# A hand-planned order of work, re-planned with measured paces, hops and buffer times, in a one-layer decoder kernel

## The chip, the cores and the metric

The kernel runs on one core of a Trainium2 chip. The metric is the device time of one execution in microseconds (us); smaller is better. The engines are TensorE (PE, matrix products into PSUM), VectorE (DVE), ScalarE (ACT), GpSimd (POOL) and SyncE (SP, which issues most DMAs). Each engine works through its own queue in order; engines wait for each other through semaphores.

## The reference

One layer of a hybrid decoder on x (256 tokens x 2048 features, float32) with 256 memory tokens:

```python
h = rmsnorm(x, norm_mix_g)
proj = h @ w_in + b_in               # GLU input | q | k | v | conv gate | attention gate
y_conv = swish(layernorm(depthwise_causal_conv31(a * sigmoid(g)))) @ w_conv_out
y_att = moba_attention(q, k, v) @ w_att_out      # 8 heads; 256 tokens are one block: plain causal
x = x + (sigmoid(g_conv) * y_conv + sigmoid(g_att) * y_att) @ w_out
x = x + cross_attention(rmsnorm(x), rmsnorm(mem), w_cq, w_ckv, w_co)      # 4 heads of 512
x = x + swiglu(rmsnorm(x), w_ffn_in, w_ffn_out)  # 5632 hidden
return rmsnorm(x, norm_final_g)
```

## The kernel before

**Products.** Every large product is made of 128-row pieces of the contraction. A value in float32 is split into hi and lo (both in the reduced form that PE multiplies at full pace), and a product of a 128x128 left piece and a 128x512 weight piece is three matmuls: hi·hi, hi·lo, lo·hi (`mm3`, lines 290 to 292). In what follows "product" means such a three.

**Blocks, units, pairs.** The work on weights is a list of blocks of 1024 output columns: glu0, glu1, k, q, v, gate10, gate11, ao0, ao1, gate00, gate01, co0, co1, wo0, wo1, cq0, cq1, ck0, ck1, cv0, cv1, xo0, xo1, ffn0 to ffn10, fo0, fo1. A block runs over pairs of contraction pieces (8 pairs; ao and co 4; fo 22). One pair of one block is a unit: 1 MB of weights, loaded by two DMAs (four for two column ranges) on SP (`load_unit`), in a buffer of 128 x 2048. A pair is of one of two kinds:
- W: 2 x 2 x 2 = 8 products. ACT casts the 2048 columns to hi, DVE subtracts to lo.
- S: the same 2x2 block product with 7 products (Winograd's form of Strassen's scheme). DVE makes sums of the weights (1024, 512 and 512 columns), ACT casts 1536 and 2048 columns, DVE subtracts as many. The left side needs sums as well (`make_extra`). S products use other PSUM banks, and `share` folds them into a result block, to which the W part is added in `finish`.

88 of 300 pairs are S: in glu1, k, q, v, gate00, gate01, wo, cq, xo two each, in ck and cv three, in ffn three and four by turns, in fo 6 and 8.

**The planner.** The program is written out by a Python planner that keeps a clock per engine: `t["pe"]`, `t["dve"]`, `t["act"]`, `t["dma"]`. `Timed` wraps DVE and ACT and adds each instruction's assumed cost to its clock; `product` adds 0.681 to PE's clock. After each product, `pump` writes out for DVE and ACT whatever, by these clocks, would start by then (`step`): tasks from a queue (evacuations, softmax and so on), the next weight step in order (`act_step`, `dve_step`), or a tap of the convolution. The order so written is the order of each engine's queue. Tasks are Python generators that yield the engine they want next, or a delay and a number of PSUM banks. PE's queue, too, holds its transposes and attention products where the planner thought that their inputs would be there.

What this planner assumes: a result is usable by another engine at the moment its cost ends; a buffer is free as soon as its release is written out (`Store.free`); a unit lands 2.0 us after a DMA clock that advances by 3.8 per unit; cost depends on the number of elements only.

**Memory.** 25 buffers of 128 x 2048 floats serve as weights (raw, hi, lo, sums) and for everything else, in pieces of a quarter, a half or a whole. `ROOM` says per block how many are kept from the weights.

**The convolution and the layer norm.** Each of 31 taps for each half of the channels is four ACT multiplications into a half buffer and one DVE addition into y (`Conv`). Taps fill idle time; they take priority if they are behind an even pace that ends at `CONV_END` = 350. Then `layer_norm` runs: sums on DVE and PE, squares and Sqrt on ACT, a reciprocal, Silu on ACT, and the split that co0 and co1 multiply. Its steps are ordinary tasks.

**The start.** `begin` loads unit 0 in four pieces; `split_first` casts and subtracts two pieces before product 0 and two before product 4. x comes in eight transposed pieces (`x_load`, `x_make`), and again by rows for the norm (`x_norm`).

Of the kernel before, what the change touches and what calls it, by code (L numbers as in the profile page):

```python
# [46 lines left out]
PRODUCT = 0.681  # L47


class Timed:  # L50
# [5 lines left out]
    def __getattr__(self, name):  # L56
        f = getattr(self._engine, name)
        if name == "dma_start":
            return f

        def call(out, *args, **kwargs):
            t, key = self._clock, self._key
            us = self._cost(math.prod(out.shape[1:]))
            t[key] = t["last"] = max(t[key], t["from"]) + us
            t["busy", key] += us
            return f(out, *args, **kwargs)  # L66
# [12 lines left out]
class Piece:  # L79
    def __init__(self, block, first, n):  # L80
        self.block, self.first, self.n = block, first, n


class Store:
# [3 lines left out]
    def __init__(self, pool, n):  # L88
        self.pool, self.n = pool, n
        self.blocks = []  # L90
        self.made = 0
# [4 lines left out]
    def take(self, n, kind):  # L96
        for b in self.blocks if n < 4 else ():
            if b["kind"] == kind:
                for f in range(0, 4, n):
                    if not any(b["used"][f : f + n]):  # L100
                        b["used"][f : f + n] = [True] * n
                        return Piece(b, f, n)
        assert self.whole() > 0, "no room"
        self.made += 1
        t = self.pool.tile([P, 4, 512], kind, tag="blk", name=f"blk_{self.made}")
        b = {"kind": kind, "tile": t, "used": [i < n for i in range(4)]}
        self.blocks.append(b)
        return Piece(b, 0, n)

    def free(self, pg):  # L110
        b = pg.block
        for x in range(pg.first, pg.first + pg.n):
            assert b["used"][x]
            b["used"][x] = False
        if not any(b["used"]):
            self.blocks.remove(b)

# [13 lines left out]
def ordered(pairs, s, how="first"):  # L131

    rest = [p for p in range(pairs) if p not in s]
    order = []
    for p in s:
        order.append(("S", p))
        if how == "turns":
            order.append(("W", rest.pop(0)))
    return order + [("W", p) for p in rest]


class Builder:
# [4 lines left out]
    def __init__(self, ctx, tc, args):  # L147
        self.tc, self.nc = tc, tc.nc
        self.t = {"pe": 0.0, "dve": 0.0, "act": 0.0, "dma": 0.0, "from": 0.0, "last": 0.0}
# [14 lines left out]
        self.seq, self.tasks, self.queue = 0, [], {"act": [], "dve": []}  # L164
        self.left, self.ready = {}, set()
# [10 lines left out]
    def take(self, n, kind=F32):  # L176
        pg = self.store.take(n, kind)
        if self.blk:
# [3 lines left out]
    def free(self, pg):  # L182
        self.store.free(pg)
# [26 lines left out]

    def run(self, task, ready=None):
        t = self.t
        t["last"] = t["from"] = t["pe"] if ready is None else ready
        try:
# [4 lines left out]
        if isinstance(cmd, str):  # L219
            heapq.heappush(self.queue[cmd], (t["last"], self.seq, task))  # L220
        else:
            delay, banks = cmd
            heapq.heappush(self.tasks, (t["last"] + delay, self.seq, banks, task))
# [22 lines left out]
    def flush(self):  # L246
        while self.tasks or any(self.queue.values()):
# [34 lines left out]
    def pe_add(self, us):  # L282
        self.t["pe"] += us
        self.t["last"] = self.t["pe"]

# [154 lines left out]
    def free_w(self, pg):  # L440
        self.held -= 1
        self.free(pg)
# [28 lines left out]
    def act_cand(self):  # L471
        if self.i_act >= len(self.acts):
            return None
        u, k = self.acts[self.i_act]
        if k == "b":
            if u not in self.sums:
                return None
            at = self.sums[u][1]
# [4 lines left out]
        return at if self.slots() >= 2 + self.owed else None  # L483

    def act_step(self):
        t = self.t
        u, k = self.acts[self.i_act]
        n = 3 if k == "a" else 4
        hi = self.take_w()
        src = self.f32(self.sums[u][0]) if k == "b" else self.f32(self.raw[u])[:, 4 - n :, :]  # L490
        self.act.copy(self.f32r(hi, 0, n), src)
        self.w[u, k] = (hi, None, n)
        self.owed += 1
        self.cast_at[u, k] = t["act"]
# [12 lines left out]
    def dve_step(self):
        t, dve = self.t, self.dve
        u, k = self.dves[self.i_dve]
        if k == "s":  # L510
            r = self.f32(self.raw[u])
            pg = self.take_w(F32)
            s = self.f32(pg)
            dve.tensor_tensor(s[:, 0:2, :], r[:, 0:1, :].to_broadcast([P, 2, 512]), r[:, 1:3, :], op=ALU.add)
            dve.tensor_tensor(s[:, 2, :], s[:, 0, :], r[:, 2, :], op=ALU.add)
            dve.tensor_tensor(s[:, 3, :], s[:, 2, :], r[:, 3, :], op=ALU.add)
            self.sums[u] = pg, t["dve"]
        else:
            hi, _, n = self.w[u, k]
            src = self.sums.pop(u)[0] if k == "b" else self.raw.pop(u)  # L520
# [3 lines left out]
            dve.tensor_tensor(self.f32r(lo, 4 - n), self.f32(src, 4 - n), self.f32(hi, 0, n), op=ALU.subtract)  # L524
            self.free_w(src)
            self.landed[u, k] = t["dve"]
            if k != "a":
                self.prepared = u + 1
        self.i_dve += 1

    def step(self, limit):
# [28 lines left out]
        if what == "task":  # L560
            self.run(heapq.heappop(self.queue[e])[2], r)
# [11 lines left out]
    def advance(self, u, k):  # L573
        while (u, k) not in self.landed:
            assert self.step(1e8), (u, k, self.units[u][0].name, self.slots())
        self.stall("w", self.landed[u, k] - self.t["pe"])

# [19 lines left out]
    def product(self, key, lhs, rhs):  # L597
# [3 lines left out]
        if n == 0:  # L601
            while self.busy[i]:
                assert self.step(1e8), key
# [3 lines left out]
        t = self.t  # L607
        t["pe"] += PRODUCT
# [4 lines left out]
    def pair_w(self, blk, u, p, how):  # L613
# [11 lines left out]
        for x, (i, t, n) in enumerate(order):  # L625
            if how == "start" and x in (0, 4):
                self.split_first(x // 4)
# [55 lines left out]
    def split_first(self, j):  # L683
        hi, lo, _ = self.w[0, "W"]
        for i in range(2):
            x = 2 * i + j
# [3 lines left out]
        if j:  # L690
            self.free_w(self.raw.pop(0))

    def begin(self):
# [9 lines left out]
        self.i_act = self.i_dve = self.n_load = 1  # L703
        self.prepared = 1
        self.load_more()

    def stream(self, blocks, on_load=None):
        self.units = [(blk, kind, p) for blk in blocks for kind, p in blk.order]
        self.acts = [(u, k) for u, (_, kind, _) in enumerate(self.units) for k in ("W" if kind == "W" else "ab")]
        self.dves = [(u, k) for u, (_, kind, _) in enumerate(self.units) for k in ("W" if kind == "W" else "sab")]  # L710
        self.raw, self.w, self.landed, self.loaded, self.cast_at, self.sums = {}, {}, {}, {}, {}, {}
        self.on_load = on_load
# [45 lines left out]
class Conv:  # L758
# [5 lines left out]
    def __init__(self, b, vt, y, t0, t1, done):  # L764
# [4 lines left out]
        self.n = 0  # L769

# [3 lines left out]
    def act_ready(self):  # L774
        if not self.todo or len(self.made) >= self.BUFS:
            return None
        return self.at.get(self.todo[0][0])

    def act_step(self):
        b = self.b  # L780
        h, j = self.todo.pop(0)
        sh = TAPS - 1 - j
        pg = None if sh == 0 else b.take(2)
# [11 lines left out]
        else:  # L795
            self.made.append((h, sh, pg, b.t["act"]))
# [4 lines left out]
    def dve_step(self):  # L801
# [4 lines left out]
        b.free(pg)  # L806
        self.n += 1
        if not self.todo and not self.made:
            b.conv = None
# [3 lines left out]
S_X = [0, 1]  # L813
# [797 lines left out]
```

## Time and profile before

| | before |
|---|---|
| time, median of 3 runs (lowest, highest) | 1761.01 us (1756.18, 1761.41) |
| the profiled execution: time, span | 1759.83 us, 1758.1 us |
| PE busy | 1687.7 us (96%) |
| DVE busy | 1479.7 us (84%) |
| ACT busy | 1013.6 us (58%) |
| HBM traffic | 351 MB, 200 GB/s over the span |
| mean granted clock of TensorE | 0.984 |

How to read it: the span runs from the first to the last instruction; the time of an execution is a little longer. A busy PE is one with a matmul in its pipeline, so short bubbles between matmuls do not show as idle. In the rows of instructions, `L66` is the wrapper line of the planner's DVE and ACT calls, so that groups there are told apart by operation and shape; `blk` is any of the 25 buffers, `psum` the PSUM tile. `[1.27 <-ACT blk L66]` behind a row means that the engine stood idle for 1.27 us before it and that an ACT instruction on `blk` ended the wait. The granted clock is a share of TensorE's full speed.

### The profile page before, as it was taken

To read this page: it belongs to the slowest core of one execution; us is meant where nothing else is said; L and a number is where in the kernel's file an instruction comes from. 1 tells how busy PE (TensorE), PEld (TensorE's weight loads), DVE (VectorE), ACT (ScalarE), POOL (GpSimd) and SP (SyncE) were. 2 spreads that over 40 slices of the span, in tenths; PEclk is the share of its full clock that TensorE was granted. 3 is DMA by queue.
4 is the path that set the end of the run, shared out by engine and by line. 5 is a ranking of instruction groups with operands and counts; after the bars stand their busy time and mean duration, and the time that the engine had idled before them with its cause. 6 is when DMAs were issued, how large, how long until landed. Compare 5 with 4: busy or idle time off the path is not lost.

```text
span 1758.1 us, 20236 instructions
## 1 busy us (share of the span) xinstructions
PE 1687.7 (96%) x7566; PEld 1385.4 (79%) x7566; DVE 1479.7 (84%) x1326; ACT 1013.6 (58%) x1064; POOL 1.4 (0%) x11
## 2 busy tenths in 40 slices
PE   8988899889999999999999999999999999999997
PEld 6876677678888888878888887888888788888776
DVE  5987789857778887898888899999898989887896
ACT  7775588764454456656555465655555555553552
POOL 0000000000000000000000000000000000000000
PEclk9999899999999999999999999999999999999999
DMA  9743364355584676554546665757566657667672
GB/s 343 259 168 132 132 203 156 120 173 174 202 284 143 234 240 205 191 177 168 192 136 201 229 204 180 253 191 246 188 222 199 221 191 275 214 217 226 209 234 90
DMA packets 129987, 352.53 MB, mean 201 GB/s; under 512 B 14433, under 2 KB 14561, under 8 KB 129889
## 3 DMA queue, kind: packets, MB, share of 16 engines
q1 hardware_dynamic: 126864, 341.11, 57.8%
q10 hardware_dynamic: 3024, 10.13, 1.5%
q8 instruction: 59, 0.97, 0.2%
q14 instruction: 40, 0.32, 0.0%
HBM read 339.65 MB, written 11.53 MB: 200 GB/s over the span
## 4 chain that ended last, share of the span: by engine, by line
PE 66%; DVE 15%; ACT 7%; issue 6%; DMA 4%; SPq 1%; DVEq 0%; ACTq 0%
PE psum L290 21%; PE psum L291 21%; PE psum L292 21%; DVE blk L66 15%; ACT blk L66 7%; DMA blk<-in_w_in 2%; PE psum L396 1%; DMA blk<-in_w_ffn_in 1%; DMA md<-blk 0%; DVE mx L66 0%; ACT L66 0%; DMA blk<-in_x 0%; SPq L455 0%; ACT junk L66 0%; SPq L456 0%
## 5 line engine op out<-in xcount | busy, mean ns | idle before, releaser
L66 DVE TENSOR_TENSOR blk<-blk,blk 128x2048 fp32r<-128x2048 f32 (+13 forms) x745 | 1105.4, 1514 | 161.0 <-ACT blk L66 142.1
L290 PE MATMUL psum<-blk,blk 128*128 128x512 f32 x2376 | 934.1, 393 | 28.5 <-DVE blk L66 23.1
L66 ACT CAST blk<-blk 128x2048 fp32r<-128x2048 f32 (+3 forms) x446 | 732.9, 1682 | 348.0 <-DVE blk L66 225.4
L291 PE MATMUL psum<-blk,blk 128*128 128x512 f32 x2376 | 925.5, 390 | 6.9 <-DVE blk L66 6.9
L292 PE MATMUL psum<-blk,blk 128*128 128x512 f32 x2376 | 924.5, 389 | 2.3 <-DVE blk L66 2.3
L290 PEld LDWEIGHTS psum<-blk,blk 128*128 128x128 f32 x2376 | 450.7, 190 | 126.1 <-DVE blk L66 26.0
L291 PEld LDWEIGHTS psum<-blk,blk 128*128 128x128 f32 x2376 | 450.8, 190 | 98.4 <-DVE blk L66 9.9
L292 PEld LDWEIGHTS psum<-blk,blk 128*128 128x128 f32 x2376 | 450.0, 189 | 95.5 <-DVE blk L66 3.6
L66 DVE TENSOR_TENSOR blk<-psum,blk 128x512 f32<-128x512 f32 (+4 forms) x249 | 188.5, 765 | 68.1 <-PE psum L292 64.0
L66 ACT ACTIVATE blk<-blk,vecs 128x256 f32<-128x256 f32 (+31 forms) x290 | 121.0, 494 | 59.2 <-DVE blk L66 55.6
L66 DVE TENSOR_TENSOR blk<-blk 128x1024 f32<-128x1024 f32 (+3 forms) x147 | 131.9, 899 | 8.8 <-DMA md<-blk 5.9
L66 ACT ACTIVATE blk<-blk,rss 128x512 f32<-128x512 f32 x30 | 21.7, 724 | 93.5 <-DVE blk L66 93.5
L66 ACT COPY blk<-psum 128x512 f32<-128x512 f32 (+2 forms) x56 | 38.9, 695 | 50.8 <-PE psum L396 41.5
L396 PE MATMUL psum<-consts,blk 128*128 128x128 f32 x312 | 46.4, 282 | 10.2 <-DVE blk L66 7.9
L396 PEld LDWEIGHTS psum<-consts,blk 128*128 128x128 f32 x312 | 36.3, 142 | 22.3 <-DVE blk L66 15.2
L66 ACT ACTIVATE junk<-blk 128x512 f32<-128x512 f32 x32 | 20.2, 630 | 51.8 <-DVE blk L66 46.6
L66 ACT ACTIVATE blk<-blk 128x512 f32<-128x512 f32 (+1 forms) x26 | 18.8, 729 | 40.0 <-DVE blk L66 35.1
L66 ACT ACTIVATE blk<-blk,rm 128x512 f32<-128x512 f32 (+1 forms) x16 | 11.6, 723 | 37.7 <-DVE blk L66 37.6
L66 ACT CAST blk<-psum 128x1024 fp32r<-128x1024 f32 (+2 forms) x30 | 20.7, 697 | 19.1 <-PE psum L396 14.5
L66 ACT ACTIVATE blk<-psum,mx 128x256 f32<-128x256 f32 (+1 forms) x24 | 10.3, 435 | 18.1 <-DVE mx L66 16.1
L66 ACT ACT_TABLE_LOAD x13 | 16.7, 1283 | 6.0 <-DVE mx L66 4.2
L66 DVE SCALAR_TENSOR_TENSOR blk<-blk,rss 128x512 f32<-128x512 f32 x22 | 16.5, 751 | 3.5 <-ACT blk L66 2.5
(66 smaller groups left out, 147.9 us busy)
## 6 DMA issues: line engine op xcount, KB each, us to landing
blk<-in_w_ffn_in SPq DMA_DIRECT2D x352, 256.0 KB, 4.3
blk<-in_w_in SPq DMA_DIRECT2D x112, 512.0 KB, 4.6
blk<-in_w_ffn_out SPq DMA_DIRECT2D x88, 512.0 KB, 5.0
blk<-in_w_ckv SPq DMA_DIRECT2D x64, 512.0 KB, 4.5
blk<-in_w_in SPq DMA_DIRECT2D x64, 256.0 KB, 5.2
blk<-in_w_out SPq DMA_DIRECT2D x32, 512.0 KB, 5.0
blk<-in_w_cq SPq DMA_DIRECT2D x32, 512.0 KB, 6.0
blk<-in_w_co SPq DMA_DIRECT2D x32, 512.0 KB, 5.6
```

Of the source, the lines that this page charges most:

```text
L66: return f(out, *args, **kwargs)
L290: mm(out, lhs[0], rhs[0], start=start, stop=False)
L291: mm(out, lhs[0], rhs[1], start=False, stop=False)
L292: mm(out, lhs[1], rhs[0], start=False, stop=stop)
L396: self.nc.tensor.transpose(out[:, 2 * c + t, :], src(c, t), self.ident)
```

## The change

The numbers of the planner, its rules, and the list of S pairs are changed. The arithmetic is not, apart from which pairs are made with seven products.

- Costs by kind of instruction, start to start; 0.15 (`HOP`) between engines; 0.12 (`AGAIN`) where an instruction reads what the one before it on its engine wrote; ACT's table loads 1.3; a product 0.6825; a DMA unit 2.5, landing at the earliest 2.6 after its issue.
- `Store` keeps for each piece and each free buffer the time at which it is really released (`at`, `rest`), and work that takes a buffer starts no earlier on the clock. The convolution holds two fixed half buffers and is asked only when the older one is free.
- The three sums of an S unit are three steps; units 1 and 2 are cast and subtracted in halves; unit 0 is split in one go ahead of everything else.
- A third queue, `low`: the steps of the layer norm, which yield to others until `LN_DUE` = 385 and go first after it. `CONV_END` is 375.
- Evacuations count results instead of trusting that (t, n) = (1, 1) is the last, and wait for what they use (`until`).
- S pairs are listed per block (`PLAN`), 94 instead of 88: gate11 one, wo1, cq1 and xo0 three, cv1 two, ffn 3 4 4 3 4 4 3 4 4 4 4. On x's side the S pairs are 2 and 3 instead of 0 and 1, and their sums are made in one go at planner time 30 (`x_extra`).
- The rows of x for the norm are loaded from planner time 14 on in steps of 2.5 (before: from 8 in steps of 3).

```diff
-PRODUCT = 0.681
+PRODUCT = 0.6825
+HOP = 0.15
+AGAIN = 0.12
+AHEAD = (0, 0, 0)
+LOOK = 1
+HALVES = 2
+SLACK = 5.0
...
         def call(out, *args, **kwargs):
             t, key = self._clock, self._key
-            us = self._cost(math.prod(out.shape[1:]))
+            us = self._cost(t, name, out, args, kwargs)
+            ins = [x for x in args if isinstance(x, bass.AP)]
+            if t[key, "wrote"] and any(overlap(t[key, "wrote"], x) for x in ins):
+                us += AGAIN
+            t[key, "wrote"] = out
...
-def dve_cost(n):
-    return 0.066 + 0.0010417 * n
+def dve_cost(t, name, out, args, kwargs):
+    n = size(out)
+    if name in ("tensor_scalar", "tensor_scalar_mul"):
+        return 0.072 + 0.00064 * n
+    if name in ("tensor_reduce", "reduce_max", "reduce_sum"):
+        return 0.1 + 0.0011 * size(args[0])
+    return 0.075 + 0.00104 * n + (0.06 if name == "scalar_tensor_tensor" else 0.0)
...
-def act_cost(n):
-    return 0.22 + 0.00057 * n if n <= 512 else 0.09 + 0.00085 * n
+def act_cost(t, name, out, args, kwargs):
+    n = size(out)
+    if name != "activation":
+        return 0.1 + 0.000835 * n
+    us = 0.183 + 0.00085 * n if n <= 256 else 0.1 + 0.00084 * n
...
+    table = TABLE.get(args[1])
+    if table and table != t["table"]:
+        t["table"] = table
+        us += 1.3
...
     def take(self, n, kind=F32):
         pg = self.store.take(n, kind)
+        self.t["from"] = max(self.t["from"], pg.at)
...
-            t["dma"] = max(t["dma"], t["pe"]) + 3.8
-            self.loaded[v] = t["dma"] + 2.0
+            t["dma"] = max(t["dma"], max(t["pe"], self.raw[v].at) + 2.6) + 2.5
+            self.loaded[v] = t["dma"]
...
+    def parts(self, u, n):
+        return [slice(0, 2), slice(2, 4)] if u <= HALVES else [slice(0, n)]
...
+        for h in self.parts(u, n):
+            self.act.copy(self.f32r(hi)[:, h, :], src[:, h, :])
...
+            if self.low[e]:
+                r = self.low[e][0][0]
+                ways.append((max(now, r) + (-0.4 if t["pe"] > self.low_due else 1.0), r, "low"))
...
     def drop_w(self, u, k):
         hi, lo, _ = self.w.pop((u, k))
-        self.free_w(hi)
-        self.free_w(lo)
+        for pg in (hi, lo):
+            self.free_w(pg, self.t["pe"] + HOP)
...
     def act_ready(self):
-        if not self.todo or len(self.made) >= self.BUFS:
+        if not self.todo or self.pages == [] or self.todo[0][0] not in self.at:
             return None
-        return self.at.get(self.todo[0][0])
+        return max(self.at[self.todo[0][0]], self.pages[0][0] if self.pages else 0.0)
...
+PLAN = {
+    "glu1": "SSWWWWWW", "k": "SSWWWWWW", "q": "SSWWWWWW", "v": "SSWWWWWW", "gate00": "SSWWWWWW",
+    "gate01": "SSWWWWWW", "wo0": "SSWWWWWW", "wo1": "SSSWWWWW", "cq0": "SSWWWWWW", "cq1": "SSSWWWWW",
+    "xo0": "SSSWWWWW", "xo1": "SSWWWWWW", "gate10": "WWWWWWWW", "gate11": "SWWWWWWW", "ck0": "SSSWWWWW",
+    "ck1": "SSSWWWWW", "cv0": "SSSWWWWW", "cv1": "SSWWWWWW", "ffn0": "SSSWWWWW", "ffn1": "SSSSWWWW",
+    "ffn2": "SSSSWWWW", "ffn3": "SSSWWWWW", "ffn4": "SSSSWWWW", "ffn5": "SSSSWWWW", "ffn6": "SSSWWWWW",
+    "ffn7": "SSSSWWWW", "ffn8": "SSSSWWWW", "ffn9": "WSSSSWWW", "ffn10": "SSSSWWWW",
+}
...
-CONV_END = 350.0
+X_EXTRA = 30.0
+X_NORM = 14.0
+CONV_END = 375.0
+LN_DUE = 385.0
```

More of the change, by code (lines that the diff above doesn't have):

```diff
@@ L180, in take, with free @@
         return pg
-    def free(self, pg):
-        self.store.free(pg)
+    def free(self, pg, at=None):
+        self.store.free(pg, self.t["last"] if at is None else at)
     def get(self, pg, lo=0, n=None):
@@ L213, in run @@
         t["last"] = t["from"] = t["pe"] if ready is None else ready
+        t["by"] = "pe" if ready is None else ""
         try:
@@ new lines, in dve_ready @@
+    def dve_ready(self, u, k, ahead):
+        more = 2 if ahead else 0
+        if k == "1":
+            if u >= self.n_load or self.slots() < 1 + self.owed + more:
+                return None
+            return max(self.loaded[u], self.store.rest[0])
+        if k in "23":
+            return self.summed.get((u, int(k) - 1))
+        if self.slots() < 1 or (u, k) not in self.cast_at:
+            return None
+        return max(self.cast_at[u, k], self.store.rest[0])
+    def dve_cand(self):
+        self.dve_at = self.pick(self.dves, self.dve_ready, max(self.t["dve"], self.t["pe"]), "dve")
+        return self.dve_at and self.dve_at[1]
@@ L559, in step @@
         was, t["from"] = t["from"], r
-        if what == "task":
-            self.run(heapq.heappop(self.queue[e])[2], r)
+        if what in ("task", "low"):
+            self.run(heapq.heappop((self.queue if what == "task" else self.low)[e])[2], r)
         elif what == "weights":
@@ L805, in dve_step, with ordered, union @@
         b.dve.tensor_tensor(yy, yy, b.f32(pg).rearrange("p j (c s) -> p (j c) s", s=S)[:, :, sh:S], op=ALU.add)
-        b.free(pg)
+        self.pages.append((b.t["dve"] + HOP, pg))
         self.n += 1
         if not self.todo and not self.made:
+            for _, pg in self.pages:
+                b.free(pg)
             b.conv = None
             b.run(self.done())
-S_X = [0, 1]
-S_MG = [0, 1]
-S_X2 = [0, 1]
-S_M = [0, 1, 2]
-S_CA = [0, 1]
-S_X3 = [0, 1, 2, 3]
+PLAN = {
[6 rows of a table added]
+}
+X_SIDE = ("glu1", "k", "q", "v", "gate10", "gate11", "gate00", "gate01")
+M_SIDE = ("ck0", "ck1", "cv0", "cv1")
+X3_SIDE = tuple(f"ffn{j}" for j in range(11))
+def ordered(name):
+    kinds = PLAN[name]
+    if name not in X_SIDE + M_SIDE + X3_SIDE:
+        return [(k, i) for i, k in enumerate(kinds)]
+    first = 2 if name in X_SIDE else 0
+    rank = [(i + first) % 8 for i in range(8)]
+    s = rank[: kinds.count("S")]
+    w = [p for p in range(8) if p not in s]
+    return [(k, (s if k == "S" else w).pop(0)) for k in kinds]
+def union(*names):
+    return sorted({p for n in names for k, p in ordered(n) if k == "S"})
 S_MID = [3, 6, 9, 12, 15, 18]
@@ L821 @@
 S_BACK = [18, 15, 12, 10, 8, 6, 4, 2]
-HOW = {}
 def setup(b):
@@ L854, in layer, with last_of, until @@
     st = {}
+    S_X = union(*X_SIDE)
+    S_MG, S_X2, S_CA = union("wo0", "wo1"), union("cq0", "cq1"), union("xo0", "xo1")
+    S_M, S_X3 = union(*M_SIDE), union(*X3_SIDE)
     half = lambda ap: ap.rearrange("p j n -> p (j n)")
+    counts = {}
+    def last_of(n, *key):
+        counts[key] = counts.get(key, 0) + 1
+        return counts[key] == n
+    def until(*keys):
+        while any(k not in b.ready for k in keys):
+            yield 0.3, 0
     by_s = lambda ap: half(ap).rearrange("p (f s) -> p f s", s=P)
+    x_kept = {}
     def x_load(p):
-        pg, t = b.page(P)
+        if p in S_X:
+            if "x" not in x_kept:
+                x_kept["x"] = b.take(2 if len(S_X) <= 2 else 4)
+            pg, t = None, b.f32(x_kept["x"])[:, S_X.index(p), :].rearrange("p (a b) -> p a b", b=P)
+        else:
+            pg, t = b.page(P)
         nc.sync.dma_start(t.rearrange("p (k t) s -> p k (t s)", k=2), a["x_t"][:, 2 * p : 2 * p + 2, :])
+        b.t["dma"] += 0.65
         return pg, t
@@ L992, in moba @@
         yield 2 + MOBA_GAP * h, 0
-        while ("kq", h // 4) not in b.ready:
-            yield 1, 0
+        yield from until(("kq", h // 4))
         yield 0, 1
@@ L1145, in evac @@
             done()
+            b.ready.add(("att", t, q))
         w = a["w_att_out"]
@@ L1287, in cross @@
     def cross(h):
+        yield from until(*((x, p) for x in "qk" for p in (2 * h, 2 * h + 1)))
         yield 1, 1
@@ L1345, in cross_out @@
     def cross_out(h):
-        while ("pt", h) not in b.ready:
-            yield 1, 0
+        yield from until(("pt", h))
         for x in range(2):
@@ L1382, in evac @@
                 act.activation(s, ps, AF.Silu, scale=r)
+                b.ready.add(("silu", j, t))
                 return
+            yield from until(("silu", j, t))
             yield "dve"
             dve.scalar_tensor_tensor(s, ps, r, s, op0=ALU.mult, op1=ALU.mult)
-            if t == 1:
+            if last_of(2, "ffn", j):
                 b.run(tr(), b.t["dve"])
```

293 lines of the change are left out of this document (180 added, 113 removed).

## The prediction

> **What bounds the kernel now.** I read the page's totals first, then the stages, then single stalls. TensorE (PE) is the bound by its total:
>
> ```profile
> span 1758.1 us, 20236 instructions
> PE 1687.7 (96%) x7566; PEld 1385.4 (79%) x7566; DVE 1479.7 (84%) x1326; ACT 1013.6 (58%) x1064; POOL 1.4 (0%) x11
> ```
>
> The 96% is an average and hides where PE waits. So I cut the span at block starts, found by counting matmuls of 512 columns (a block of eight pairs with s S pairs is 64-s products of three matmuls). The view of windows gives, after the times, busy us of PE, PEld, DVE, ACT and POOL, then granted clock, DMA share and GB/s:
>
> ```profile
> 6.08:57.86 51.78, 47.63 (x192) 37.82 (x193) 39.08 (x44) 40.23 (x58) 0.00 (x0) 0.93 0.91 334
> 57.86:391.58 333.72, 296.70 (x1270) 238.85 (x1268) 271.31 (x270) 237.63 (x392) 0.00 (x0) 0.94 0.49 164
> 391.58:519.42 127.84, 127.84 (x565) 105.89 (x564) 95.92 (x71) 60.11 (x40) 0.00 (x0) 1.00 0.64 222
> 519.42:1037.87 518.45, 510.77 (x2410) 422.70 (x2409) 439.86 (x400) 292.05 (x282) 0.00 (x0) 1.00 0.57 191
> 1037.87:1510.42 472.55, 465.99 (x2095) 384.66 (x2094) 434.88 (x356) 259.65 (x192) 0.00 (x0) 1.00 0.64 217
> 1510.42:1758.05 247.63, 234.58 (x1023) 191.54 (x1021) 197.79 (x186) 120.98 (x98) 0.00 (x0) 0.98 0.62 199
> ...
> 1086.00:1127.69 41.69, 41.69 (x189) 34.61 (x188) 39.17 (x30) 22.72 (x15) 0.00 (x0) 1.00 0.62 215
> ...
> 1339.55:1383.30 43.75, 41.93 (x189) 34.59 (x188) 41.28 (x34) 23.34 (x16) 0.00 (x0) 1.00 0.62 204
> ```
>
> The third row is the yardstick. From ao0 to gate01 there are 32+32+62+62 = 188 products and nothing else on PE: 127.84/188 = 0.680 us each, with no wait at all. ffn1 (the row from 1086.00) has 60 products, 40.8 us, and one wide transpose: 0.88 us for that, 0.11 for each block of 128 columns. With these two prices every other stage splits into work and loss:
> - glu0 (6.08 to 57.86): 64 products, 43.5; lost 8.3.
> - glu1 to gate11 (57.86 to 391.58): 376 products, 255.7; six wide transposes, 5.3; eight attention heads of 15 column blocks, 13.2; column sums, 0.5. Sum 274.7; lost 59.0.
> - co0 to xo1: 680 products, 462.4; 20 wide transposes, 17.6; cross attention and its sums, 25.4. Lost 13.
> - ffn0 to ffn10: 666 products, 452.9; some 12 wide transposes, 10.6. Lost 9.
> - fo0 and fo1: 338 products, 229.8; the last matmul is at 1747.8. Lost 6.6, then a tail of 10.3.
>
> So 96 us are lost, 67 of them before 391.58, and there DVE is busy for only 81% (271.31 of 333.72): no engine is full, yet PE waits. One of those stalls, instruction by instruction (the timeline of ACT, DVE and PE; in brackets the idle time before and who ended it):
>
> ```profile
> 99.61 3.25 ACT L66 ACTIVATE blk<-blk,vecs 128x248 f32<-128x248 f32 x8 [3.34 <-DVE blk L66]
> 102.77 3.68 ACT L66 CAST blk<-blk 128x2048 fp32r<-128x2048 f32 x2
> ...
> 104.68 2.29 DVE L66 TENSOR_TENSOR blk<-blk,blk 128x2048 fp32r<-128x2048 f32 x1 [3.81 <-ACT blk L66]
> ...
> 107.62 0.80 PE L290 MATMUL psum<-blk,blk 128*128 128x512 f32 x1 [5.06 <-DVE blk L66]
> ```
>
> Two taps of the convolution (columns 248 and 247) stand ahead of a weight cast in ACT's queue and wait 3.34 us for a page that DVE has not yet released. DVE then waits 3.81 us for the cast, and PE 5.06 us for DVE. No work is short; the order is wrong, because the planner believes a page to be free as soon as its release is written down. Two more stalls of this kind, and the first and last of the six groups into which PE's waits from 80 to 365 fall (us in total, times, longest; the six add up to 36.3):
>
> ```profile
> 157.14 0.80 PE L290 MATMUL psum<-blk,blk 128*128 128x512 f32 x1 [4.34 <-DVE blk L66]
> ...
> 217.50 0.80 PE L290 MATMUL psum<-blk,blk 128*128 128x512 f32 x1 [7.69 <-DVE blk L66]
> ...
> PE psum L290 <- DVE blk L66: 19.2, 4, 7.7
> ...
> PE psum L291 <- DVE blk L66: 1.8, 1, 1.8
> ```
>
> Such stalls also cost more than themselves:
>
> ```profile
> 292.22 0.95 PE L1027 MATMUL psum<-consts,blk 128*128 128x128 f32 x3 [1.92 <-DVE blk L66]
> ...
> 292.42:295.82 3.40, 3.40 (x11) 2.87 (x11) 2.84 (x4) 2.89 (x8) 0.00 (x0) 0.50 0.17 69
> ```
>
> After a wait of 1.92 us the granted clock is 0.50 for the next 3.40 us, in which eleven matmuls do work of half that time. So of the 59 us lost some 36 are waits, and most of the rest I put down to half clock.
>
> **The change part by part.** Six products less: 6 x 0.680 = 4.1 us less of PE, certain. Their price lies on DVE and ACT, by these groups (mean ns after the busy us):
>
> ```profile
> L66 DVE TENSOR_TENSOR blk<-blk,blk 128x2048 fp32r<-128x2048 f32 x299 | 675.0, 2287 | 112.8 <-ACT blk L66 105.9 <-PE psum L291 4.3 <-DMA blk<-in_x_t 1.1
> L66 ACT CAST blk<-blk 128x2048 fp32r<-128x2048 f32 x299 | 561.2, 1908 | 247.5 <-DVE blk L66 177.7 <-PE psum L291 48.6 <-PE psum L292 17.7
> L66 DVE TENSOR_TENSOR blk<-blk,blk 128x1536 fp32r<-128x1536 f32 x88 | 154.1, 1751 | 6.4 <-ACT blk L66 5.9 <-PE psum L291 0.6
> L66 DVE TENSOR_TENSOR blk<-blk,blk 128x512 f32<-128x512 f32 x218 | 150.0, 691 | 9.3 <-ACT junk L66 2.5
> L66 ACT CAST blk<-blk 128x1536 fp32r<-128x1536 f32 x88 | 130.2, 1479 | 42.6 <-PE psum L291 16.6 <-PE psum L292 11.0 <-DVE blk L66 8.7
> L66 DVE TENSOR_TENSOR blk<-blk 128x1024 f32<-128x1024 f32 x88 | 107.2, 1218 | 7.4 <-DMA md<-blk 5.9 <-PE psum L292 1.4
> L66 DVE TENSOR_TENSOR blk<-psum,blk 128x1024 f32<-128x1024 f32 x29 | 35.5, 1224 | 1.0
> ```
>
> A W pair costs DVE one subtraction, 2.29 us. An S pair costs sums of 1.22 + 2 x 0.69 and subtractions of 1.75 + 2.29, together 6.64: 4.35 more. ACT pays 1.48 more. Six pairs: 26 us of DVE. gate11, so far without S, also gets a result block: share() and four additions, about 5.4 us. One more left pair in each of merged, x2 and cross output wants its differences, by the same groups under 2 us each. All of it lies beside PE while DVE has room: the ffn blocks go from 434.88 of 472.55 us to 447.9 of 470.5, 95%. Bounds there: nothing, and 8 four-S blocks out of the last ten each losing what 1339.55 lost (43.75 - 40.8 - 0.88 = 2.1), 16.6.
>
> First weights. ACT and DVE at the start, PE's waits, and the landing time of the second unit's four pieces:
>
> ```profile
> 8.03 0.91 ACT L66 ACTIVATE blk<-blk,vecs 128x256 f32<-128x256 f32 x2 [1.48 <-DMA blk<-in_x_t]
> 8.97 1.66 ACT L66 CAST blk<-blk 128x512 fp32r<-128x512 f32 x3
> 12.54 4.22 ACT L66 CAST blk<-blk 128x512 fp32r<-128x512 f32 x3 [1.90 <-DVE blk L66]
> ...
> 15.02 0.51 PE L290 MATMUL psum<-blk,blk 128*128 128x512 f32 x1 [1.27 <-ACT blk L66]
> 17.34 0.79 PE L291 MATMUL psum<-blk,blk 128*128 128x512 f32 x1 [1.82 <-DVE blk L66]
> ...
> blk<-in_w_in SPq DMA_DIRECT2D x4, 256.0 KB, 5.1
> ```
>
> The second half of unit 0 is cast only at 8.97, behind x's second pair, which waits 1.48 us for its DMA. Then the extra forms of x pair 1 hold ACT (idle 1.90, then their cast at 12.54) before unit 1's cast, though unit 1, its last piece issued at 5.46, has landed at 10.6. The change splits unit 0 ahead of everything, takes x's extra forms away to planner time 30, and casts units 1 and 2 in halves. Unit 1's first half is then ready at about 10.6 + 0.95 + 1.1 = 12.7 at the latest, when unit 0's eight products end (6.1 + 5.4 + 0.5 = 12.0). Halving costs 2 x 1.22 - 2.29 = 0.15 for each pair of instructions, hidden here. Of 8.3 us lost I take 7 off (bounds 0 and 8.3); the half-clock stretch goes with the stalls. The loads themselves are issued in the same order on SP; the eight rows of x for the norm move from planner time 8-29 to 14-31.5, needed at 43 by glu0's results, so they stay covered.
>
> Order in glu1 to gate11. The convolution keeps two fixed pages and is asked only when the older one is free; casts carry the time of their buffer; the three sums become three steps, so an evacuation can go between; the layer norm becomes a filler until 385, its convolution may end at 375. Is there DVE time for it? Until co0 DVE must do 39.08 + 271.31 + 95.92 + 4.35 + 5.4 = 416 us. My forecast gives it 513.3 - 0.7 - 7 - 46 = 459.6, so 90.5% busy. In the ffn stage it runs at 92.0% (434.88 of 472.55) with 1.9% lost. At that rate 6 of the 59 would stay; I take 13, since taps and attention heads cross between engines more often than ffn does. Bounds: 6, and 37 from the rival below. What is late next is DVE itself. The layer norm's place is one of the stalls:
>
> ```profile
> 356.45 1.28 ACT L66 ACT_TABLE_LOAD   x1 [1.33 <-DVE blk L66]
> ...
> 359.25 1.22 PE L1041 MATMUL psum<-blk,blk 128*128 128x256 f32 x2 [4.37 <-ACT blk L66]
> ```
>
> Its Silu, with a table load of 1.28, stood in ACT's queue ahead of the copy that the last attention head needed. As a filler due at 385 it starts after the heads; it still issues every instruction that it has now, and what waits for it is co0 alone, which moves from 519.42 to about 466, some 80 us behind the due time. If that cover were gone, co0 would wait for whatever is left of it.
>
> By the Trainium skill, page "TensorE: Matmul & The Clock Gate", section "Why this matters for your kernels", only idle gaps over about 3 us drop the clock; the row above shows it after 1.92, so the trace is stricter. By the page the leftover 13 would be about 9, and the time 1693; that lies inside the forecast's own span and gets no chance of its own.
>
> The split sums also help in ffn:
>
> ```profile
> 1362.34 1.42 DVE L66 TENSOR_TENSOR blk<-blk,blk 128x512 f32<-128x512 f32 x2
> 1363.67 2.67 DVE L66 TENSOR_TENSOR blk<-psum,blk 128x512 f32<-128x512 f32 x3
> ...
> 1364.41 0.66 PE L396 MATMUL psum<-consts,blk 128*128 128x128 f32 x4 [1.82 <-DVE blk L66]
> ```
>
> Here an evacuation stood behind sums; between two of them it could start 1.42 earlier. Against the fuller DVE I take 9 to 7 in ffn (bounds 0, and 9 + 16.6 = 25.6), and 13 to 9 in co0 to xo1 (bounds 0, and 13 + 14 = 27 if two more pairs and three sets of differences lie wholly bare); in fo, whose S pairs stay, 1 off (bounds 0 and 6.6).
>
> Sum: 4.1 + 7 + 46 + 4 + 2 + 1 = 64.1, so a span of 1694.0. The profiled run took 1759.83, 1.7 more than its span, and the median 1761.01, 1.2 more again: 1697. All best ends together would give 1758.1 - 94 + 2.9 = 1667; I don't expect them at once and let the range begin at 1677.
>
> **The rivals.**
> *DVE is the bound in the first third.* If it gets no fuller before co0 than in co0 to xo1 (439.86 of 518.45, 84.8%), 416 us take 491 instead of 513.3: 22.6 saved there, with 3.4 for the five later products and 7 elsewhere a span of 1725, a median near 1728. For it: DVE waits for ACT in 105.9 us of the 2048 groups. Against: ffn's 92%.
>
> *Slower: starved of blocks.* Convolution pages, y and its kin stay later, and a load waits for a free block already:
>
> ```profile
> SPq L453 <- PE psum L292: 481.6, 104, 17.5
> ```
>
> If in gate11 to gate01 (32 pairs) no second unit fits, a pair takes landing 5.1 + 1.91 + 2.29 = 9.3 instead of 5.4, 3.9 more, and its wait brings the half clock, some 1.7 more. From 64/5.6 = 12 pairs on the change loses; 20 pairs cost 112, giving 1809. Against: SP's waits there end without PE losing anything in 391.58 to 519.42.
>
> *No effect.* The order that comes out is not better in fact, since real waits differ from the planner's; new stalls replace old ones, and the median stays near 1761.
>
> **How the numbers follow.** Forecast (1677 to 1720) 0.64; DVE bound (1720 to 1750) 0.20; no effect 0.05; slower 0.09; still faster than 1677, 0.02. Range 1677 to 1738, which leaves out about 0.2. Within 0.3% (5 us, what a measurement here can tell) is 0.05, faster 0.86, slower 0.09.
>
> **What would show it.** After: x2306 products; the clock 1.00 in nearly every window from 60 to 390; ACT's waits for DVE ahead of convolution taps gone; ao0's first product near 338 instead of 391.58; DVE at 90% until co0; no PE wait over 1 us before 20. I am wrong if DVE sits at 80% there with PE still waiting, if half-clock windows appear in ffn, or if new waits of SP end late in gate00.

## The result, and the profile after

The changed kernel takes 1667.86 us (median of four runs, 1667.44 to 1668.41) against 1760.97 for the kernel before: a ratio of 0.9477, 95% interval 0.9461 to 0.9494. That is 93 us less, where 64 were forecast, and 9 us below the low end of the range. The profiled execution took 1668.15 us, 1.85 more than its span.

The page of the kernel after, totals:

```profile
span 1666.3 us, 20283 instructions
PE 1650.7 (99%) x7548; PEld 1371.1 (82%) x7548; DVE 1506.4 (90%) x1367; ACT 1029.4 (62%) x1078; POOL 1.4 (0%) x11
```

PE went from 96% to 99% of a shorter span. The same six stages as in the prediction, cut at the same block starts, in the view of windows of the kernel after (columns as there: busy us of PE, PEld, DVE, ACT, POOL, then granted clock, DMA share, GB/s), with glu1 alone behind them:

```profile
6.05:51.35 45.30, 44.85 (x192) 35.80 (x193) 34.91 (x38) 37.49 (x56) 0.00 (x0) 1.00 1.04 386
51.35:328.83 277.48, 275.01 (x1263) 227.84 (x1262) 262.50 (x264) 229.59 (x372) 0.00 (x0) 1.00 0.56 193
328.83:458.13 129.30, 129.30 (x570) 106.41 (x569) 114.62 (x94) 77.36 (x66) 0.00 (x0) 1.00 0.65 228
458.13:963.23 505.10, 504.84 (x2404) 422.90 (x2403) 451.13 (x421) 298.15 (x291) 0.00 (x0) 1.00 0.57 196
963.23:1424.79 461.56, 461.56 (x2087) 383.25 (x2086) 442.36 (x365) 262.85 (x193) 0.00 (x0) 1.00 0.65 220
1424.79:1666.30 241.51, 230.97 (x1024) 190.99 (x1022) 200.07 (x189) 121.12 (x98) 0.00 (x0) 0.99 0.63 208
...
51.35:97.08 45.73, 43.63 (x196) 35.57 (x195) 45.37 (x39) 39.96 (x53) 0.00 (x0) 1.00 0.55 191
```

With the prediction's own prices (0.680 us for a product, 0.88 for a wide transpose, and so on) each stage again splits into work and loss:

| stage | lost before | forecast to stay | lost after |
|---|---|---|---|
| glu0: 64 products, 43.5 | 8.3 | 1.3 | 1.8 |
| glu1 to gate11: 375 products, 255.0, and 18.5 of transposes and attention | 59.0 | 13 | 4.0 |
| ao0 to gate01: 188 products, 127.8, and 0.5 of column sums | 0 | 0 | 1.0 |
| co0 to xo1: 678 products, 461.0, and 43.0 | 13 | 9 | 1.1 |
| ffn: 663 products, 450.8, and 10.6 | 9 | 7 | 0.2 |
| fo: 338 products, 229.8, and one wide transpose, 0.9 (last matmul at 1655.3) | 6.7 | 5.6 | 0 |

(The layer norm's column sums, four matmuls, stand in the row of ao0 to gate01: they moved there with the layer norm. The prediction's line on fo leaves out the one wide transpose there, eight matmuls of 128 columns; with it the rows give 6.7, its 6.6 within rounding.) Of 96 us lost, 8 are left. Those 88, the 4.1 of the six products, and a tail that grew by 0.7, which counts against them, come to 91.4 of the 91.8 us by which the span shrank.

All groups of PE's waits that the view of waits lists for the kernel after (us in total, times, longest):

```profile
PE psum L341 <- DVE blk L79: 2.1, 2, 1.3
PE psum L1695 <- POOL consts L985: 1.4, 1, 1.4
PE psum L342 <- DVE blk L79: 0.6, 3, 0.3
PE psum L341 <- ACT blk L79: 0.5, 1, 0.5
PE psum L1222 <- ACT blk L79: 0.4, 1, 0.4
```

Five us in all, no single wait over 1.4; the first group, two waits, lies in glu1. The groups of the products' matmuls and of DVE's subtractions in the kernel after (count, busy us, mean ns, idle time before them and what ended it):

```profile
L341 PE MATMUL psum<-blk,blk 128*128 128x512 f32 x2306 | 904.4, 392 | 2.6 <-DVE blk L79 2.1 <-ACT blk L79 0.5
...
L79 DVE TENSOR_TENSOR blk<-blk,blk 128x2048 fp32r<-128x2048 f32 x297 | 671.4, 2286 | 60.6 <-ACT blk L79 59.4 <-DMA blk<-in_w_att_out 0.3
...
L79 DVE TENSOR_TENSOR blk<-blk,blk 128x1536 fp32r<-128x1536 f32 x94 | 164.6, 1751 | 2.3 <-ACT blk L79 2.2
```

x2306 is the count that the prediction named. One subtraction costs what it did (2286 ns against 2287): no instruction became faster. What fell is the idle time before it, 112.8 to 60.6 us.

### The profile page after: what moved, and what is told of

The parts are those of the page before. It is cut to its first block, busy times and chain, and to the rows that moved or that the text cites. A ratio compares the mean times of both kernels' runs of the same rounds, so it can differ in the third digit from the quotient of the medians.

```text
span 1666.3 us, 20283 instructions
## 1 busy us (share of the span) xinstructions
PE 1650.7 (99%) x7548; PEld 1371.1 (82%) x7548; DVE 1506.4 (90%) x1367; ACT 1029.4 (62%) x1078; POOL 1.4 (0%) x11
## 4 chain that ended last, share of the span: by engine, by line
PE 94%; ACT 2%; DVE 2%; DMA 2%; issue 0%; SPq 0%; DVEq 0%; ACTq 0%
PE psum L342 30%; PE psum L341 30%; PE psum L343 30%; PE psum L447 2%; DVE blk L79 2%; ACT blk L79 2%; DMA blk<-in_w_in 1%; DMA vecs<-in_vecs 0%; ACT L79 0%; PE psum L1222 0%; PE psum L1182 0%; PE psum L1208 0%; PE psum L1462 0%; PE psum L1223 0%; PE psum L1181 0%
## 5 line engine op out<-in xcount | busy, mean ns | idle before, releaser
L79 DVE TENSOR_TENSOR blk<-blk,blk 128x2048 fp32r<-128x2048 f32 (+9 forms) x773 | 1126.5, 1490 | 89.7 <-ACT blk L79 79.6
L79 ACT CAST blk<-blk 128x2048 fp32r<-128x2048 f32 (+3 forms) x458 | 745.8, 1667 | 350.2 <-DVE blk L79 240.7
L341 PE MATMUL psum<-blk,blk 128*128 128x512 f32 (+1 forms) x2370 | 922.6, 389 | 2.6 <-DVE blk L79 2.1
L342 PE MATMUL psum<-blk,blk 128*128 128x512 f32 (+1 forms) x2370 | 916.4, 387 | 0.6 <-DVE blk L79 0.6
L343 PE MATMUL psum<-blk,blk 128*128 128x512 f32 (+1 forms) x2370 | 916.0, 386 | 0.0
L341 PEld LDWEIGHTS psum<-blk,blk 128*128 128x128 f32 x2370 | 445.3, 188 | 92.7 <-DVE blk L79 1.7
L342 PEld LDWEIGHTS psum<-blk,blk 128*128 128x128 f32 x2370 | 445.4, 188 | 90.4 <-DVE blk L79 2.6
L343 PEld LDWEIGHTS psum<-blk,blk 128*128 128x128 f32 x2370 | 445.1, 188 | 90.7 <-DVE blk L79 0.4
L79 DVE TENSOR_TENSOR blk<-psum,blk 128x512 f32<-128x512 f32 (+4 forms) x254 | 191.9, 764 | 44.7 <-PE psum L343 40.5
L79 DVE TENSOR_TENSOR blk<-blk 128x1024 f32<-128x1024 f32 (+3 forms) x155 | 140.8, 910 | 3.0 <-PE psum L343 1.4
L447 PE MATMUL psum<-consts,blk 128*128 128x128 f32 x312 | 40.5, 272 | 0.0
L79 ACT ACTIVATE blk<-blk 128x512 f32<-128x512 f32 (+1 forms) x26 | 18.4, 726 | 21.5 <-DVE blk L79 21.4
L79 DVE SCALAR_TENSOR_TENSOR blk<-blk,rx,blk 128x512 f32<-128x512 f32 x28 | 20.4, 747 | 0.5
```

Of the source, the lines that this page charges most:

```text
L341: mm(out, lhs[0], rhs[0], start=start, stop=False)
L342: mm(out, lhs[0], rhs[1], start=False, stop=False)
L343: mm(out, lhs[1], rhs[0], start=False, stop=stop)
L447: self.nc.tensor.transpose(out[:, 2 * c + t, :], src(c, t), self.ident)
```

## The experiments

Kernels named before_ are edits of the kernel before, the others of the kernel after. Times are medians; ratios are to the kernel before, with their 95% intervals.

**The two main theories.** One: the time at which a buffer is really released does most of it (it names the stall at 99.61 in the prediction). The other: the paces and hops do, since they act in every stage. Each was undone alone.

```diff
 # no_buffer_times: a buffer counts as free when its release is written out
+        at = 0.0
...
-        self.pages.append((b.t["dve"] + HOP, pg))
+        self.pages.append((0.0, pg))
```

> The changed kernel (1667.9 us), whose planner again takes every buffer and both convolution pages as free at once. Theory A (buffer times carry the gain): taps again stand ahead of weight casts in ACT's queue and wait for their page, so 25 to 45 us come back between 50 and 330 us, with half-clock stretches: about 1700. Theory B (paces and hops carry it): under 5 us come back, 1668 to 1673.

Measured 1705.57 us, 0.9697 (0.9678 to 0.9715): 37.7 us given back. The timeline of this kernel shows the old stall again:

```profile
186.44 4.67 ACT L79 ACTIVATE blk<-blk,vecs 128x233 f32<-128x233 f32 x12 [2.93 <-DVE blk L79]
...
191.02 3.26 ACT L79 CAST blk<-blk 128x2048 fp32r<-128x2048 f32 x2
...
192.94 2.29 DVE L79 TENSOR_TENSOR blk<-blk,blk 128x2048 fp32r<-128x2048 f32 x1 [3.70 <-ACT blk L79]
...
199.40 0.68 DVE L79 TENSOR_TENSOR blk<-psum,blk 128x512 f32<-128x512 f32 x1
...
200.14 0.79 PE L342 MATMUL psum<-blk,blk 128*128 128x512 f32 x1 [8.04 <-DVE blk L79]
```

Three taps (twelve multiplications) stand ahead of a cast, the first of them waits 2.93 us for a page, DVE waits 3.70 for the cast, and PE resumes 8.04 us late, as the evacuation behind that work ends. The stage from glu1 to gate11 of this kernel, and the stretch around that restart (windows):

```profile
51.20:364.90 313.70, 288.21 (x1263) 232.96 (x1261) 266.78 (x265) 231.25 (x377) 0.00 (x0) 0.96 0.50 171
195.60:205.80 10.20, 5.66 (x13) 4.27 (x14) 9.92 (x13) 0.00 (x0) 0.00 (x0) 0.50 0.01 4
```

313.70 us against 277.48 in the kernel after: 36.2 of the 37.7 lie in this one stage, the one with the convolution. Elsewhere undoing them costs next to nothing: 1.4 us in fo.

```diff
 # no_hops_old_costs
-PRODUCT = 0.6825
-HOP = 0.15
-AGAIN = 0.12
+PRODUCT = 0.681
+HOP = 0.0
+AGAIN = 0.0
 # and dve_cost, act_cost as before, by the number of elements alone
```

> The changed kernel with the old costs by number of elements, no hop between engines, no cost of a dependent instruction, and 0.681 per product; buffer times stay. Theory A: little comes back, 1668 to 1678. Theory B: the planner thinks DVE 60 us less busy than it is, falls out of step wherever DVE is full, and 30 us or more come back: 1698 or more.

Measured 1738.46, 0.9885 (0.9869 to 0.9901): 70.6 given back. So the second theory weighs more, and the two halves of this edit were then taken apart.

> The changed kernel with HOP and AGAIN at 0, costs by kind kept. With the old costs too it lost 71 us. If hops are the larger share, 1705 to 1735; if the costs by kind are, 1670 to 1690.

> The changed kernel with the old costs by number of elements and 0.681 per product, hops kept. If hops are the larger share, 1672 to 1690; if the costs are, 1705 to 1735. Table loads (16 of 1.28 us) and short reductions are then unknown to the planner, so the loss should lie around the attention heads and the layer norm, not in ffn.

`no_hops` (HOP and AGAIN 0, not tried apart; costs by kind kept): 1718.42, 0.9773 (0.9756 to 0.979), 50.6 given back. `old_costs` (hops kept): 1686.06, 0.9594 (0.958 to 0.9608), 18.2. The two add up to 68.8 of 70.6. Cut at the block starts of `old_costs`, 9.6 of its 18.2 lie in glu1 to gate11 and 2.8 in ffn, roughly where its expectation put them; but another 4.6 lie in co0 to xo1. Where hops matter, by windows of `no_hops` for glu1 to gate11, co0 to xo1 and ffn:

```profile
52.00:341.70 289.70, 281.19 (x1263) 227.80 (x1262) 267.06 (x264) 229.28 (x377) 0.00 (x0) 0.99 0.54 187
471.30:992.00 520.70, 512.14 (x2404) 422.97 (x2403) 452.52 (x421) 296.20 (x288) 0.00 (x0) 1.00 0.55 192
992.00:1475.10 483.10, 468.94 (x2086) 384.98 (x2086) 447.27 (x367) 264.94 (x196) 0.00 (x0) 0.99 0.62 212
```

They are 12.2, 15.6 and 21.5 us longer than in the kernel after. In its view of waits the largest group is PE before wide transposes:

```profile
PE psum L447 <- DVE blk L79: 10.6, 11, 1.9
```

Eleven times PE reached a transpose whose input DVE had not written; the planner had taken it for finished. Eight of these waits, 9.6 us, lie in ffn. In the kernel after no such group is left. This is the kind of wait, up to 1.9 us at a time, that the prediction saw at 1364.41 and put down to the order of sums and evacuation alone.

A larger hop was tried as well:

> The changed kernel with a hop of 0.20 instead of 0.15. If its planner is near the truth, small errors cost little: 1668 to 1675. If 0.15 is a lucky value, 1680 or more.

`HOP` = 0.2: 1672.27, 0.9503 (0.9487 to 0.9519), 4.4 slower than 0.15. That is less than the 8 us that `before_product`, below, moves by with no cause found, so it does not show that 0.15 is best; it shows that a third too much costs little beside leaving out `HOP` and `AGAIN`.

`HOP` is not a delay of 0.15 us in the trace. The planner's costs run from start to start and are shorter than the instructions themselves: it takes 0.955 for a cast of 1024 columns, which lasts 1.05 (timeline of the kernel after):

```profile
13.35 1.05 ACT L79 CAST blk<-blk 128x1024 fp32r<-128x1024 f32 x1 [1.09 <-DMA blk<-in_w_in]
...
14.44 2.54 DVE L79 TENSOR_TENSOR blk<-blk,blk 128x1024 fp32r<-128x1024 f32 x2 [0.92 <-ACT blk L79]
```

The cast ends at 14.40 and DVE starts 0.04 later, 1.09 after the cast's start; 0.955 + 0.15 is 1.105. So about 0.1 of the 0.15 is the end of the instruction itself, which the next one on the same engine need not wait for (in the rows of `no_buffer_times` above, ACT's cast starts at 191.02, 0.09 before its taps end), and 0.04 is the handover.

**From the other end.** `neither` undoes buffer times, hops, costs, the load clock, the three-step sums, the halves, the layer norm's queue and the six pairs; the early split of unit 0, x's S pairs 2 and 3, the waits by count and the convolution's two fixed half buffers stay. The next three add parts back, still with 88 pairs.

> The changed kernel with all of this undone: buffer times, hops, costs by kind, the old clock of the loads, sums in one step, layer norm at once, no halves, 88 pairs. What stays is the split of unit 0 ahead, x's pairs 2 and 3, and waits by count. If the undone parts hold the gain, it is back at the kernel before: 1750 to 1770. If what stays holds a part of it, clearly less.

> As 'neither', but with buffer times. If the two causes add, it lies 38 us below 'neither' (what their removal cost in the changed kernel). If buffer times help only on true paces, within 10 us of 'neither'.

> As 'neither', but with costs by kind, hops and the price of a dependent instruction. If the causes add, 71 us below 'neither', 1680 to 1695. If true paces are worth less while buffers are taken as free at once, 1700 to 1730, with ACT waiting for pages ahead of taps as before.

> As 'neither', with both. It differs from the changed kernel by 88 pairs (9 us by the run before), the layer norm at once (4), the old clock of the loads, sums in one step and no halves. If these last three are small, 1678 to 1688; if each is worth as much as the two big ones, over 1695.

| | us | ratio (95%) |
|---|---|---|
| neither | 1736.57 | 0.987 (0.9855 to 0.9884) |
| buffer times only | 1714.61 | 0.9749 (0.9734 to 0.9764) |
| paces and hops only | 1711.72 | 0.9731 (0.9717 to 0.9746) |
| both | 1692.1 | 0.9619 (0.9603 to 0.9635) |

Added alone they bring 22.0 and 24.9, together 44.5: nearly a sum, but well below the 38 and 71 of the expectations. `both` is still 24.2 slower than the kernel after. The six pairs and the layer norm, undone one at a time below, cost 13.4 together; the other 10.8 would be the clock of the loads, the sums in three steps, the halves, and whatever all these do together, which was not taken apart. Windows of `buffer_times_only`, glu1 to gate11 and co0 to xo1:

```profile
55.90:354.20 298.30, 283.13 (x1270) 227.74 (x1269) 274.05 (x272) 238.92 (x391) 0.00 (x0) 1.00 0.54 182
482.10:1001.30 519.20, 511.25 (x2410) 422.68 (x2409) 440.04 (x399) 291.81 (x282) 0.00 (x0) 1.00 0.56 191
```

and the same two of `paces_hops_only`, with ffn behind them:

```profile
53.10:359.10 306.00, 285.43 (x1270) 231.16 (x1269) 270.58 (x269) 232.49 (x382) 0.00 (x0) 0.98 0.52 175
488.60:999.50 510.90, 507.97 (x2409) 425.23 (x2408) 439.59 (x401) 290.82 (x282) 0.00 (x0) 1.00 0.58 195
999.50:1464.96 465.46, 464.17 (x2095) 384.79 (x2094) 433.68 (x356) 262.72 (x194) 0.00 (x0) 1.00 0.64 219
```

With buffer times alone, co0 to xo1 is as long as before (519.20 against 518.45); with paces and hops alone it is 7.6 shorter, and ffn, with the pairs of before, 7.1 shorter than before (465.46 against 472.55). That agrees with the undoings. Taken from the kernel after, the same parts cost more (37.7 and 70.6) than they bring alone. DVE is fuller there, and a wrong order may have less slack to hide in; no run shows that this is why.

**The pairs and the full DVE.**

> The changed kernel with the old counts of S pairs (88). If DVE has room for the six pairs, the six products come back whole: 6 x 0.68 = 4.1 us, 1672. If the fuller DVE costs stalls that eat the gain, 1668 or less.

`pairs_88` (the old list of S pairs in the kernel after): 1676.97, 0.9533 (0.9518 to 0.9549), 9.1 slower, more than either expectation. Six products are 4.1 of it. Most of the rest is one stall in ck0 that this order has and the other has not (timeline, then window, of this kernel):

```profile
691.75 0.50 PE L342 MATMUL psum<-blk,blk 128*128 128x512 f32 x1 [2.21 <-DVE blk L79]
```

```profile
692.40:695.80 3.40, 3.40 (x10) 2.66 (x9) 3.40 (x2) 3.40 (x3) 0.00 (x0) 0.50 1.02 408
```

2.21 us of wait and 3.40 us at half clock, which loses 1.7: 3.9 together.

```diff
 # ffn_all_four: ffn0, ffn3 and ffn6 too
-"ffn0": "SSSWWWWW", "ffn3": "SSSWWWWW", "ffn6": "SSSWWWWW",
+"ffn0": "SSSSWWWW", "ffn3": "SSSSWWWW", "ffn6": "SSSSWWWW",
```

> The changed kernel with four S pairs in every ffn block (ffn0, 3 and 6 get one more; 97 in all). DVE stands at 96% there. If DVE still has room, three products less: 2 us, 1666. If it is full, each further pair costs its 4.35 us of DVE less 0.68: 11 us, 1679, with waits of PE for DVE spread over the ffn blocks.

Measured 1680.58, 0.9563 (0.9548 to 0.9577), 12.7 slower. Its ffn stage:

```profile
964.85:1437.76 472.91, 464.95 (x2077) 380.60 (x2076) 454.56 (x377) 266.50 (x195) 0.00 (x0) 1.00 0.65 217
```

DVE is busy for 454.56 of 472.91 us, 96%, as in the kernel after (442.36 of 461.56, 96%): that is full. Three more pairs put 12.2 us more on DVE, and the stage grew by 11.3 although PE has 2.0 less to do. So in ffn a fuller DVE costs nothing until about 96%, and then almost everything. (Of the 12.7 us, 2.4 lie in glu1, far from the edit: any edit re-plans the whole order.)

**The layer norm and smaller suspects.**

```diff
 # ln_at_once: the layer norm's steps are ordinary tasks
-        yield "dve.low"
+        yield "dve"
...
-CONV_END = 375.0
-LN_DUE = 385.0
+CONV_END = 350.0
+LN_DUE = -1.0
```

> The changed kernel with the convolution due at 350 and the layer norm's steps as ordinary tasks. If the layer norm's place is worth what its stall was before (4.5 us and the half clock behind it, 2), it costs 5 to 10 us: 1673 to 1678. If good costs alone keep it harmless, 1668 to 1671.

Measured 1672.18, 0.951 (0.9493 to 0.9527), 4.3 slower, nearly all of it one stall in ao0 (timeline, then window, of this kernel):

```profile
337.80 0.50 PE L342 MATMUL psum<-blk,blk 128*128 128x512 f32 x1 [2.68 <-DVE blk L79]
```

```profile
338.30:341.70 3.40, 3.40 (x9) 2.67 (x9) 3.33 (x5) 2.40 (x2) 0.00 (x0) 0.51 0.84 302
```

Three edits of the kernel before:

```diff
 # before_fixed_pages: the convolution keeps two half buffers, clocks as before
+            self.pages = [b.take(2) for _ in range(self.BUFS)]
 # before_conv_375
-CONV_END = 350.0
+CONV_END = 375.0
 # before_product
-PRODUCT = 0.681
+PRODUCT = 0.6825
```

> The kernel before with one part of the change alone: the convolution keeps two half buffers for good instead of taking a new one for each tap; the planner's clocks are as before. 'neither' was 23 us faster than the kernel before, 18 of it in glu1 to gate11. If a newly taken buffer's real readers were what taps waited for, 15 to 20 us go: 1740 to 1745. If not, 1757 to 1763, and the 23 us come from the start and the other small parts.

> The kernel before with the convolution due at 375 instead of 350. If spreading the convolution were the point, 10 us or more faster. If order by wrong clocks decides, within 15 us of 1760 in either direction.

> The kernel before with one number changed: 0.6825 instead of 0.681 for a product, 0.2%, nearer to nothing real. If its order is planned on wrong clocks and lands by accident, the time moves by 5 to 25 us in either direction. If the kernel before is 23 us worse for a definite reason, it stays within 5 us of 1760.

Fixed pages 1762.9, 1.0021 (1.0005 to 1.0038); `CONV_END` 1761.83, 1.0017 (1.0008 to 1.0027): nothing gained by either. But 0.2% on the assumed length of a product took some 8 us off: 1751.06, 0.9951 (0.9936 to 0.9966), though 0.6825 is no nearer to the measured 0.680 than 0.681 was. A plan made with wrong clocks can move by that much with no cause that a run shows.

**What stays open.** `neither` is some 23 us faster than the kernel before (1.3%), though nearly everything is undone in it. x's side was put back too:

> 'neither' (1736.6 us) with x's S pairs 0 and 1 again, their sums at planner time 20 and the rows for the norm from 8 on in steps of 3. If the order of x holds the 23 us, 1755 to 1765. If it does not, within 8 us of 1737.

`neither_old_x` (x's S pairs 0 and 1, their sums at 20, rows of x from 8 in steps of 3): 1750.79, 0.995 (0.9935 to 0.9965). That holds 14 of the 23. The other 9 are as large as what `before_product` moved by. By its block starts, 4.8 of them lie in glu0 (47.0 us against 51.8), where the early split of unit 0 acts; that split was not tried alone, and neither were the waits by count.

## Why the prediction was wrong

**The direction and the mechanism held.** Nearly all of the 59 us of the first third were misplaced order, not missing work; a stall like the one that the prediction read at 99.61 comes back when buffer times are undone. In the stretch of the convolution ACT's waits for DVE, view of waits of the kernel before from 58 to 392, then of the kernel after from 51 to 330:

```profile
ACT blk L66 <- DVE blk L66: 76.9, 32, 9.8
```

```profile
ACT blk L79 <- DVE blk L79: 26.0, 24, 3.2
```

They fell to a third. The prediction's sign had them gone; taps still wait up to 3.2 us for a page. What is gone is PE's wait behind them; from k to gate11 the view of waits gives PE 0.4 us in all.

**Terms that came out.** Six products: x2306, 4.1 us. The start: 8.3 to 1.8, 6.5 against the 7 taken; once the products run, PE waits only twice before 20, at its first two matmuls (timeline of the kernel after):

```profile
6.13 0.50 PE L341 MATMUL psum<-blk,blk 128*128 128x512 f32 x1 [0.54 <-ACT blk L79]
6.86 0.50 PE L342 MATMUL psum<-blk,blk 128*128 128x512 f32 x1 [0.22 <-DVE blk L79]
```

DVE until co0: 34.91 + 262.50 + 114.62 = 412.0 of 452.1 us, 91%, where 416 and 90.5% were forecast. Half clock is gone: 1.00 in every stage up to fo.

**The step that failed is what stays.** The prediction kept 13 us in the first third, 9 in co0 to xo1, 7 in ffn and 5.6 in fo; 4.0, 1.1, 0.2 and nothing were measured. These four differences add up to 29.5, against the 27.7 us by which the span came out below the forecast 1694.0; the 1.0 lost from ao0 to gate01, the tail's 0.7 and the start's 0.5 go the other way. Two errors are in it.

First, ffn was its yardstick for a full DVE: "at that rate 6 of the 59 would stay". But ffn's 1.9% was not the price of a DVE at 92%. It was the same fault in a milder form. `paces_hops_only`, with the pairs of before, cut ffn's loss from 9 to 2 with DVE at 93% (433.68 of 465.46), and that of co0 to xo1 by more than half; the kernel after runs ffn at 96% DVE with 0.2 lost. `ffn_all_four` shows where the true edge lies in ffn. The first third thus kept less than the 6 that the prediction gave as its least.

Second, the prediction gave the new hops and costs no term of their own after gate11: it priced there only the split sums against the fuller DVE, 2 + 4 + 1 us. Undoing the hops alone costs 50.6 us, 37 of it in co0 to xo1 and ffn. Its reading of the wait at 1364.41, an evacuation behind sums, may hold for that row (the split sums were not tried alone), but waits at transposes come back with the hops undone although the sums stay split.

**The low end.** The prediction worked out "all best ends together" as 1667 and did not expect them at once. They came nearly at once, because they were not independent: wrong clocks of the same planner stood behind most of them, and the change corrected those clocks together (`no_hops` alone brings losses back in three stages). That the sum lies 0.9 us from the measured median is partly luck: the first third kept 4.0 where 6 was its best, the start 1.8 where 0 was.

**fo** is the term with the least explained. From its first product to its last it takes 237.3 us in the kernel before, 235.8 in `neither`, and 230.5 in the kernel after, in `buffer_times_only` and in `no_hops` alike; `paces_hops_only` has 232.2 and `no_buffer_times` 231.9. So buffer times alone remove this loss, paces and hops alone most of it. In `neither` most of it is five short waits of PE, 3.2 us together, the longest 1.28; why buffer times end them was not followed up.

**The rivals.** "DVE is the bound in the first third", 0.20, is refuted for the stage: it runs with DVE at 262.50 of 277.48 us, 95%, and loses 4.0. That DVE would sit at 85% had been taken from a stage whose idle time was misplanned. In one block DVE is the bound all the same: in glu1 it is busy for 45.37 of 45.73 us, PE waits 2.1 us for it, and the block takes 1.9 longer than in the kernel before (windows of that kernel):

```profile
57.86:101.72 43.86, 43.35 (x195) 35.66 (x194) 39.08 (x31) 33.62 (x52) 0.00 (x0) 1.00 0.58 204
```

DVE has 6.3 us more to do there than before. Of the 4.0 us that the stage still loses, 2.7 lie in this block (62 products, 42.2, and one wide transpose).

"Starved of blocks" is refuted by ao0 to gate01: 129.30 of 129.30 us busy. The layer norm as a filler brought 4.3; the wait that the prediction showed at 359.25 was 4.37, but in `ln_at_once` the loss falls elsewhere, in ao0.

**The clock.** The Trainium skill, "TensorE: Matmul & The Clock Gate", section "Why this matters for your kernels", has the clock fall after idle gaps over about 3 us. The runs again show it sooner: 0.50 after a wait of 2.21 in `pairs_88` and 0.51 after one of 2.68 in `ln_at_once`, for 3.40 us each, beside the 1.92 of the prediction. The length of the wait alone does not decide it, though: another wait of 1.92 us in the kernel before left the clock at 1.00 (timeline, then window):

```profile
1064.55 0.50 PE L292 MATMUL psum<-blk,blk 128*128 128x512 f32 x1 [1.92 <-DVE blk L66]
```

```profile
1062.00:1066.00 4.00, 2.08 (x8) 1.43 (x9) 3.97 (x4) 3.74 (x6) 0.00 (x0) 1.00 0.35 86
```

## What to carry to other kernels

When a statically ordered program loses time in many places, look for one wrong assumption of the planner before pricing the places one by one; if they share a cause, their best ends come together and the range must reach there. Do not take a stage's loss at high load as the price of that load unless its order is known to be right; push the load until it hurts instead. Give the planner what lies between its own end of an instruction and the start of what depends on it on another engine: 0.15 us here, which left out with the 0.12 of `AGAIN` cost 3% of this kernel.

## What the runs showed of the hardware that was not expected

DVE can be kept at 96% for the 462 us of ffn with PE at its pace beside it (0.2 us lost); at 99%, over the 46 us of glu1, PE waited 2.1 us for it. The time from a result's planned end to its use on another engine, 0.15 us in this planner, is no rounding error for an order written ahead: with it taken as zero, together with the 0.12 for an instruction that reads what its predecessor wrote, the same arithmetic took 50.6 us longer.
